# A hybrid decoder layer on one core: a convolution head as a pair in seven products, attention's second halves inside the next pairs, later transposes in block 1

## The chip, the core and the metric

The kernel runs on one core of a Trainium2 chip. The metric is the device time of one execution in microseconds (us). Before the change it is 1216.02 us, the median of three runs (1215.99 to 1218.19).

## The reference

One layer for 512 tokens of 1024 features, all in float32: a feed-forward block, a mixer of two branches (dilated attention and a gated linear recurrence), and a second feed-forward block. Cut to the parts that matter here:

```python
h = h + 0.5 * rms_norm(swiglu(rms_norm(h, g1), w_gate, w_up, w_down), g2)     # first feed-forward block
u = rms_norm(h, mix_norm_pre)
q, k, v, xr, yr, gl = split(u @ w_in)          # 3 x 1536, 1024, 1024, 2048 columns
# attention: 3 groups (dilation 1, 4, 16) of 4 heads of 128; the groups are merged by their log-sum-exp
alpha = softmax(stack(lses), axis=0)
attn_d = einsum('gbsh,gbshe->bshe', alpha, stack(outs)) @ w_attn_branch
# recurrence: causal convolution of width 4 per channel, two gates per head of 256 channels, linear scan
rec_d = (rg_lru_branch(xr, conv_w, conv_b, ...) * gelu(yr)) @ w_rec_branch
gates = sigmoid(gl)
h = h + rms_norm((gates[0] * attn_d + gates[1] * rec_d) @ w_out, mix_norm_post)
h = h + 0.5 * rms_norm(swiglu(rms_norm(h, g3), ...), g4)                      # second feed-forward block
```

## The kernel before

**Precision.** Every large product is made of three matmuls. A weight arrives by DMA in a `raw` buffer, and `split` makes a high half of it on ScalarE (ACT, `L294`) and the remainder, the low half, on VectorE (DVE, `L295`). The activations are split in the same way. High times high, high times low and low times high are added up in PSUM (`L307` to `L309`, or `L677` to `L679` in a pair).

**Pairs in seven products.** Two column blocks of 128 outputs with the same input can be computed as a 2 x 2 block product with seven products in place of eight. Each of the seven has 256 columns, four steps over the features and three matmuls a step: 84 matmuls of 128x256, where the two blocks by themselves take 48 of 128x512. `w_forms` makes the sums of weights that this needs, `seventh` issues one product, `seven` and `seven_on` issue all seven with the evictions that combine them. In `seven` the sums are built outside PSUM, in the order p1, p2, p6, p5, p7, p4, p3; in `seven_on`, in the order p1, p5, p6, p2, p7, p3, p4, several products are built on a copy of an earlier one in PSUM (`copy`, `L691`), so a product can wait for an eviction.

**Stages.** The layer runs through: first feed-forward block; `block1`, which finishes it for one block of 128 tokens at a time (residual, norm statistics, the row `u`, and with `bd1.turn(b)` eight transposes into `um`); the values of attention (`values_first` for group 0, `values_two` for groups 1 and 2 in seven products, whose weight sums are made by `add` at `L1134`); then for each head the three pairs of queries and keys (`qk`, groups 0 to 2) and `attend`; four pairs of output gates; the attention's output product; the recurrence's stage in the order of `LRU_ORDER` (branch 0, branch 1, conv 0, branch 2, gates 0, conv 1, branch 3, ...); the output products; and the second feed-forward block.

**`attend`.** Its first half makes scores, their maxima and exponentials for three groups, and one `exchange` (a masked product, a small matmul with the constant `same` at `L1296`, a masked sum) of group 0's maxima and sums. A row of small VectorE operations makes the weight of each group (`L1304` to `L1315`). The second half begins with a second `exchange` of group 0's weight, scales the exponentials, transposes them (`L1322`) and multiplies them with the values (`om`).

**Conv.** A head has two blocks of 128 channels. Today each is a `gemm` of its own, copied into the padded row `xr` and convolved with four taps (one on ACT, three on DVE).

**Order.** A scheduler puts the instructions of each engine in order by the priority that they had when they were traced; `tc.high_priority(offset)` moves a piece ahead by a number of steps (`AHEAD` 100 for weight loads and splits, `EVAC` 200 for evictions). Each engine then runs its own list in order and waits on semaphores. Weight buffers: `raw` has 2, `w8` (128x1024, both halves) 4, `w4` (128x512) 2. PSUM has 5 tiles `acc` and 3 tiles `aux`. Weights come in the order of `stream_plan`, two 1 MB loads ahead.

Of the kernel before, what the change touches and what calls it, by code (L numbers as in the profile page):

```python
# [10 lines left out]
F32 = mybir.dt.float32  # L11
# [23 lines left out]
EVAC = 200  # L35
NFIRST = 5
# [13 lines left out]
PAIRED = tuple(("branch", h) for h in range(4))  # L50
# [130 lines left out]
def hybrid_layer(ctx: ExitStack, tc: tile.TileContext, xT: bass.AP, xN: bass.AP, wst: bass.AP,  # L181
# [489 lines left out]
    def seventh(t, w, p, ps, start):  # L671
        if len(t[p][0].shape) == 4:
            ps = ps.rearrange("q (b t) -> q b t", b=2)
        for k in range(4):
            ks = slice(k * P, (k + 1) * P)
            wh, wl, xh, xl = w[p][:, 0, ks], w[p][:, 1, ks], t[p][0][:, k], t[p][1][:, k]
            PE.matmul(ps, wh, xh, start=start and k == 0, stop=False, skip_group_check=True)  # L677
            PE.matmul(ps, wh, xl, start=False, stop=False, skip_group_check=True)  # L678
            PE.matmul(ps, wl, xh, start=False, stop=k == 3, skip_group_check=True)  # L679
# [30 lines left out]
    def seven(t, w, z, g, u, seen=lambda ap: ap):  # L710


        b, y = acc_ps()[:, :HB], acc_ps()[:, :HB]

        def product(p, ps, start):
            seventh(t, w, p, ps, start)

        def copy(ps):
            c = tpool.tile([P, HB], F32, name="c", tag="c", bufs=CB)
            with tc.high_priority(offset=EVAC):  # L720
                ACT.activation(c, ps, AF.Copy)  # L721
            return c

        def sum_of(dst, ps, c):
            with tc.high_priority(offset=EVAC):
                DVE.tensor_add(dst, seen(ps), seen(c))
# [339 lines left out]
    def block1(b, sums):  # L1066
        bd1.block(b, sums)
        if b >= 2:
            bd1.turn(b - 2)
# [12 lines left out]
    with ExitStack() as mx:  # L1082
# [16 lines left out]
        def values_first():  # L1099
# [4 lines left out]
            for b in range(4):  # L1104
                bl = slice(b * P, (b + 1) * P)
                for k in range(KC):
                    wh, wl = (w.rearrange("p (k c) -> p k c", k=2)[:, k % 2, :] for w in ws[k // 2])
                    PE.matmul(pss[b], um.hi[k][:, bl], wh, start=k == 0, stop=False)
# [110 lines left out]
        def qk(hd):  # L1219

            q, k = [], []
            for g in range(NG):
                w = pair_of(("pair",) + pairs[hd][g])
                tq, tk = (apool.tile([P, T], F32, name="qk", tag="qk", bufs=QKB) for _ in range(2))
                if g == 0:
                    seven(t, w, acc_ps()[:, :HB], *([nat(x)[:, 2 * i:2 * i + 2] for i in range(2)] for x in (tq, tk)),
                          seen=lambda ap: ap.rearrange("q (p b r) -> q p b r", p=2, b=4))
                else:
                    seven(t, w, acc_ps()[:, :HB], *([x[:, h] for h in HALVES] for x in (tq, tk)))
# [10 lines left out]
        def attend(hd, heads):  # L1240
# [49 lines left out]
            def exchange(dst, src, n):  # L1290
# [5 lines left out]
                PE.matmul(ps, same, x, start=True, stop=True)  # L1296
# [19 lines left out]
            w0 = apool.tile([P, 4, 1], F32, name="w0", tag="w0", bufs=2)  # L1316
            exchange(w0, e[:, 0:1, :], 1)

            def transposed(i, blocks):
                ps, o = aux_ps(), 0  # L1320
                for b in blocks:
                    PE.transpose(ps[:, o:o + P], b, ident)  # L1322
                    o += P
                t = facc[:, i, :]
                ACT.activation(t[:, :o], ps[:, :o], AF.Copy)
                return t

            pts = []
            for g in (1, 2):
                pv = pg[g - 1]  # L1330
                DVE.tensor_mul(pv, pv, e[:, g, :, None].to_broadcast([P, 4, P]))
                pts.append(transposed(3 + g, [pv[:, b, :] for b in range(4)]))
            for b in range(4):
                DVE.tensor_scalar(win[b], win[b], w0[:, b, :], None, op0=ALU.mult)
            ta = transposed(6, [p0[0][:, i * P:(i + 1) * P] for i in range(3)])
            tb = transposed(7, [p0[1][:, i * P:(i + 1) * P] for i in range(4)])
            om = aux_ps()
            for g in (1, 2):
                for b in range(4):
                    PE.matmul(om[:, b * P:(b + 1) * P], vt[g][:, b, :], pts[g - 1][:, b * P:(b + 1) * P],  # L1340
                              start=g == 1 and b == 0, stop=False, skip_group_check=True)
            on = pbr(om)
            for i, (b, j) in enumerate(((0, 0), (1, 0), (1, 1), (2, 1), (2, 2), (3, 2), (3, 3))):
                t = (ta if i < 3 else tb)[:, (i % 3 if i < 3 else i - 3) * P:][:, :P]
                PE.matmul(on[:, :, b, :], vt[0][:, j, :], t.rearrange("q (p r) -> q p r", p=4),
                          start=False, stop=i == 6, skip_group_check=True)
            ACT.activation(attn.hi[hd], om, AF.Copy)
            DVE.tensor_sub(attn.lo[hd], om, attn.hi[hd].bitcast(F32))
# [21 lines left out]
    with ExitStack() as mx:  # L1370
# [48 lines left out]
        def two_tiles(w, g, u):  # L1419

            lo, hi = HALVES

            def up(dst, ps, sign):
                with tc.high_priority(offset=EVAC):
                    ACT.activation(dst[:, lo], ps, AF.Copy, scale=sign)

            def g1(ps, c):
                with tc.high_priority(offset=EVAC):
                    DVE.tensor_add(g[:, hi], ps, c)

            def u1(ps, c):
                with tc.high_priority(offset=EVAC):
                    DVE.scalar_tensor_tensor(u[:, hi], ps, -1.0, c, op0=ALU.mult, op1=ALU.subtract)

            seven_on(t, w, lambda y: up(g, y, 1.0), g1, lambda v: up(u, v, -1.0), u1)

        def conv(hd, then):

            for c in (2 * hd, 2 * hd + 1):
                ps, w = acc_ps(), fetch(("in", 36 + c))  # L1440
                if c % 2:
                    then()
                gemm(ps, w, um)
                xr = lpool.tile([P, 3 + T], F32, name="xr", tag="xr", bufs=2)
                DVE.memset(xr[:, 0:3], 0.0)
                xc = sig[:, c, :]
                with tc.high_priority(offset=EVAC):
                    DVE.tensor_copy(ip(xr[:, 3:]), pi(ps))
# [4 lines left out]
                    split(rec.hi[c], rec.lo[c], xc)  # L1453

        gels, late = {}, []

        def branch(hd):

            gels[hd] = []
            if ("branch", hd) in PAIRED:  # L1460
                w = paired.pop(("branch", hd))
                gels[hd] = [lpool.tile([P, T], F32, name="ge", tag="ge", bufs=8) for _ in range(2)]
                two_tiles(w, *gels[hd])
# [75 lines left out]
        for i, (what, hd) in enumerate(LRU_ORDER):  # L1539
            if i and LRU_ORDER[i - 1] == PAIRED[-1]:  # L1540
# [197 lines left out]
```

## Time and profile before

| | before |
|---|---|
| median of 3 runs | 1216.02 us |
| the profiled execution | 1215.6 us |
| its span, first to last instruction | 1213.8 us |
| granted TensorE clock, mean | 0.998 |
| busy: PE, PEld, DVE, ACT, POOL | 1203.8, 1103.0, 1012.5, 802.5, 26.1 us |
| pair matmuls of 128x256 (`L677` to `L679`) | 3 x 1288 |
| convolution, branch and gate matmuls of 128x512 (`L307` to `L309`) | 3 x 128 |

PE is TensorE's matmul, PEld its weight load, which overlaps it; DVE is VectorE, ACT ScalarE, POOL GpSimd, and SPq the queue of SyncE, which issues most loads. Matmuls are pipelined: a row's duration covers more than the distance to the next row's start, and the distance is what a matmul costs. In a row of the profile "idle before" names the wait that ended last. An `x2` or `x4` behind a row stands for as many instructions of the same kind in succession.

### The profile page before, as it was taken

To read this page: it belongs to the slowest core of one execution; us is meant where nothing else is said; L and a number is where in the kernel's file an instruction comes from. 1 tells how busy PE (TensorE), PEld (TensorE's weight loads), DVE (VectorE), ACT (ScalarE), POOL (GpSimd) and SP (SyncE) were. 2 spreads that over 40 slices of the span, in tenths; PEclk is the share of its full clock that TensorE was granted. 3 is DMA by queue.
4 is the path that set the end of the run, shared out by engine and by line. 5 is a ranking of instruction groups with operands and counts; after the bars stand their busy time and mean duration, and the time that the engine had idled before them with its cause. 6 is when DMAs were issued, how large, how long until landed. Compare 5 with 4: busy or idle time off the path is not lost.

```text
span 1213.8 us, 19596 instructions
## 1 busy us (share of the span) xinstructions
PE 1203.8 (99%) x7838; PEld 1103.0 (91%) x7838; DVE 1012.5 (83%) x1547; ACT 802.5 (66%) x1377; POOL 26.1 (2%) x51
## 2 busy tenths in 40 slices
PE   9999999999999999999999999999999999999997
PEld 8899999999888999999989888888899999999996
DVE  7988888899689888888766899875798888889975
ACT  7556778776566565666735888834566677878752
POOL 0000000000011000000000000000100000000000
PEclk9999999999999999999999999999999999999999
DMA  6223333334635222222222441325443333333341
GB/s 248 102 73 122 122 122 122 122 122 146 242 119 162 70 96 88 79 99 85 100 75 87 144 169 70 105 104 180 149 140 122 122 122 122 122 122 122 139 174 70
DMA packets 29835, 148.75 MB, mean 123 GB/s; under 512 B 3376, under 2 KB 6832, under 8 KB 15792
## 3 DMA queue, kind: packets, MB, share of 16 engines
q1 hardware_dynamic: 22176, 130.04, 30.2%
q0 software_dynamic: 7280, 17.30, 4.3%
q8 instruction: 61, 1.00, 0.3%
q14 instruction: 30, 0.25, 0.1%
q10 hardware_dynamic: 288, 0.17, 0.0%
HBM read 137.01 MB, written 6.29 MB: 118 GB/s over the span
## 4 chain that ended last, share of the span: by engine, by line
PE 92%; DVE 4%; ACT 2%; DMA 1%; issue 1%; DVEq 0%; ACTq 0%
PE acc L677 15%; PE acc L678 15%; PE acc L679 15%; PE acc L308 6%; PE acc L307 6%; PE acc L309 6%; PE aux L946 3%; PE aux L947 3%; PE aux L948 3%; PE acc L423 3%; PE acc L422 3%; PE acc L421 3%; DVE w L295 1%; DMA raw<-in_w 1%; ACT w L294 1%
## 5 line engine op out<-in xcount | busy, mean ns | idle before, releaser
L677 PE MATMUL acc<-big,w 128*128 128x256 f32 x1288 | 365.4, 284 | 0.3 <-ACT c L691 0.3
L678 PE MATMUL acc<-big,w 128*128 128x256 f32 x1288 | 365.4, 284 | 0.0
L679 PE MATMUL acc<-big,w 128*128 128x256 f32 x1288 | 365.0, 283 | 0.0
L295 DVE TENSOR_TENSOR w<-raw,w 128x1024 fp32r<-128x1024 f32 (+1 forms) x274 | 298.9, 1095 | 60.7 <-ACT w L294 55.2
L294 ACT ACTIVATE w<-raw 128x1024 fp32r<-128x1024 f32 (+1 forms) x274 | 260.5, 955 | 98.1 <-PE acc L309 37.8
L677 PEld LDWEIGHTS acc<-big,w 128*128 128x128 f32 x1288 | 246.9, 192 | 2.5 <-ACT c L691 0.9
L678 PEld LDWEIGHTS acc<-big,w 128*128 128x128 f32 x1288 | 246.9, 192 | 1.6
L679 PEld LDWEIGHTS acc<-big,w 128*128 128x128 f32 x1288 | 246.9, 192 | 0.0
L946 PE MATMUL aux<-w,xf 128*128 128x512 f32 x196 | 76.3, 393 | 0.8 <-ACT w L294 0.8
L947 PE MATMUL aux<-w,xf 128*128 128x512 f32 x196 | 76.6, 391 | 0.0
L948 PE MATMUL aux<-w,xf 128*128 128x512 f32 x196 | 76.3, 389 | 0.0
L294 ACT ACTIVATE w<-s 128x1024 fp32r<-128x1024 f32 x53 | 56.1, 1058 | 19.6 <-PE acc L679 15.6
L295 DVE TENSOR_TENSOR w<-s,w 128x1024 fp32r<-128x1024 f32 x53 | 64.6, 1219 | 3.0 <-ACT w L294 2.9
L640 DVE TENSOR_TENSOR s<-raw 128x512 f32<-128x512 f32 x53 | 36.4, 687 | 32.8 <-DMA raw<-in_w 32.8
L691 ACT ACTIVATE c<-acc 128x256 f32<-128x256 f32 x78 | 29.6, 381 | 39.0 <-PE acc L679 38.6
L307 PE MATMUL acc<-big,w 128*128 128x512 f32 x128 | 49.8, 389 | 0.0
L308 PE MATMUL acc<-big,w 128*128 128x512 f32 x128 | 49.8, 389 | 0.0
L309 PE MATMUL acc<-big,w 128*128 128x512 f32 x128 | 49.8, 389 | 0.0
L854 ACT ACTIVATE g<-g 128x256 f32<-128x256 f32 x35 | 14.6, 416 | 50.1 <-DVE g L853 50.1
L721 ACT ACTIVATE c<-acc 128x256 f32<-128x256 f32 x72 | 27.2, 379 | 29.3 <-PE acc L679 27.9
L307 PE MATMUL acc<-xf,w 128*128 128x512 f32 (+1 forms) x136 | 46.3, 343 | 0.0
L309 PE MATMUL acc<-xf,w 128*128 128x512 f32 (+1 forms) x136 | 46.2, 340 | 0.0
(428 smaller groups left out, 2804.3 us busy)
## 6 DMA issues: line engine op xcount, KB each, us to landing
raw<-in_w SPq DMA_DIRECT2D x107, 1024.0 KB, 4.8
raw<-in_w SPq DMA_DIRECT2D x16, 512.0 KB, 3.5
big<-xf POOLq DMA_DIRECT2D x6, 512.0 KB, 3.3
gains<-in_rows POOLq DMA_DIRECT2D x5, 512.0 KB, 5.2
h<-in_x SPq DMA_DIRECT2D x8, 256.0 KB, 4.9
h<-in_xn POOLq DMA_DIRECT2D x4, 512.0 KB, 5.4
kept_m<-h POOLq DMA_DIRECT2D x4, 512.0 KB, 2.9
vals<-in_w SPq DMA_DIRECT2D x2, 1024.0 KB, 7.1
```

The costliest lines, as they stand in the source:

```text
L294: ACT.activation(dh, src, AF.Copy)
L295: DVE.tensor_sub(dl, src, dh.bitcast(F32))
L307: PE.matmul(ps, wh, xh, start=first, stop=False)
L308: PE.matmul(ps, wh, xl, start=False, stop=False)
L309: PE.matmul(ps, wl, xh, start=False, stop=last)
L421: PE.matmul(ps, x.hi[k][:, bl], wh, start=k == 0, stop=False)
L677: PE.matmul(ps, wh, xh, start=start and k == 0, stop=False, skip_group_check=True)
L678: PE.matmul(ps, wh, xl, start=False, stop=False, skip_group_check=True)
L679: PE.matmul(ps, wl, xh, start=False, stop=k == 3, skip_group_check=True)
L946: PE.matmul(ps, xh, wh, start=first and j == 0, stop=False, skip_group_check=True)
L947: PE.matmul(ps, xh, wl, start=False, stop=False, skip_group_check=True)
L948: PE.matmul(ps, xl, wh, start=False, stop=j == 1, skip_group_check=True)
```

## The change

Three edits go together.

1. `PAIRED` gets `("conv", 0)`: both blocks of the convolution's head 0 come from one `seven_on` pair, whose parts are written straight into the two padded rows `xr`; both blocks' taps follow the pair. Conv 1 to 3 stay as they were. The condition on `LRU_ORDER[i - 1]` names `("branch", 3)` outright, so it selects the same place.
2. `attend` returns its second half as the function `rest`, and `seven` calls it in the middle of a later pair by its new argument `then`: head 0's after p1 of group 1 of head 1's pairs, head 1's and 2's after p4 of group 0 of the next head's, head 3's after p4 of the first pair of output gates. The first half is traced at priority offset `FRONT` (60), the second at `BACK` (150), and the second exchange's matmul is issued behind the last product matmul traced so far (`state["last"]`).
3. `block1` calls `bd1.turn(0)` only at block 2, and no longer `turn(1)` at block 3; `values_first` calls `turn(1)`, `turn(2)`, `turn(3)` after the second of eight steps of its blocks 0, 1, 2 (before: `turn(2)` and `turn(3)` in blocks 1 and 2).

```diff
+BACK = 150
+FRONT = 60
...
-PAIRED = tuple(("branch", h) for h in range(4))
+PAIRED = tuple(("branch", h) for h in range(4)) + (("conv", 0),)
...
-            PE.matmul(ps, wl, xh, start=False, stop=k == 3, skip_group_check=True)
+            state["last"] = PE.matmul(ps, wl, xh, start=False, stop=k == 3, skip_group_check=True).ins
...
-    def seven(t, w, z, g, u, seen=lambda ap: ap):
+    def seven(t, w, z, g, u, seen=lambda ap: ap, then={}):
...
             seventh(t, w, p, ps, start)
+            if p in then:
+                then[p]()
...
-        if b >= 2:
-            bd1.turn(b - 2)
+        if b == 2:
+            bd1.turn(0)
...
-                    if k == 1 and 0 < b < 3:
+                    if k == 1 and b < 3:
                         bd1.turn(b + 1)
...
-                PE.matmul(ps, same, x, start=True, stop=True)
+                with tc.issue_after(behind) if behind else nullcontext():
+                    PE.matmul(ps, same, x, start=True, stop=True)
...
-            exchange(w0, e[:, 0:1, :], 1)
+            def rest():
+                with tc.high_priority(offset=BACK):
+                    weighted()
+            def weighted():
+                w0 = apool.tile([P, 4, 1], F32, name="w0", tag="w0", bufs=2)
+                exchange(w0, e[:, 0:1, :], 1, state["last"])
...
         for hd in range(NH):
-            attend(hd, qkvs.pop(hd))
+            with tc.high_priority(offset=FRONT):
+                rest = attend(hd, qkvs.pop(hd))
             if hd + 1 < NH:
-                qkvs[hd + 1] = qk(hd + 1)
+                qkvs[hd + 1] = qk(hd + 1, {0: {"p4": rest}} if hd else {1: {"p1": rest}})
...
             seven(t, pair_of(("pair", 52 + c, 53 + c)), acc_ps()[:, :HB], [g[:, h] for h in HALVES],
-                  [u[:, h] for h in HALVES])
+                  [u[:, h] for h in HALVES], then={} if c else {"p4": rest})
...
+            if ("conv", hd) in PAIRED:
+                then()
+                xrs = [padded() for _ in cs]
+                two_tiles(paired.pop(("conv", hd)), *([ip(xr[:, 3:])[:, 2 * h:2 * h + 2, :] for h in range(2)]
+                                                      for xr in xrs),
+                          seen=lambda ap: ap.rearrange("q (p i) -> q p i", p=2))
+                for c, xr in zip(cs, xrs):
+                    convolved(c, xr)
+                return
```

The order of the instructions moves with it at three places of which the prediction speaks. Line numbers of the changed kernel are 4 to 34 higher (the split is `L298` and `L299`, an eviction in a pair `L695`, the value sums `L1140`, a combination in `seven` `L732`).

VectorE at the beginning of the second values; `w8_3974` is the first weight's low half, `vals` the weight sums, `big_4029` and `rb_4025` forms of the activations. Before:

```order
L617 SCALAR_TENSOR_TENSOR ts_3987<-facc_79,ts_3986 128x1024
L618 TENSOR_TENSOR facc_79<-facc_79 128x2x512
L295 TENSOR_TENSOR big_4029<-ts_3986,big_4029 128x1024
L295 TENSOR_TENSOR rb_4025<-ts_3987,rb_4025 128x1024
L295 TENSOR_TENSOR w8_3974<-raw_3960,w8_3974 128x1024
L1134 TENSOR_TENSOR vals_3790<-vals_3964,vals_3966 128x1024
L295 TENSOR_TENSOR w8_3980<-raw_3962,w8_3980 128x1024
```

Now:

```order
L621 SCALAR_TENSOR_TENSOR ts_3987<-facc_79,ts_3986 128x1024
L622 TENSOR_TENSOR facc_79<-facc_79 128x2x512
L299 TENSOR_TENSOR big_4029<-ts_3986,big_4029 128x1024
L1140 TENSOR_TENSOR vals_3774<-vals_3964,vals_3966 128x1024 x2
L299 TENSOR_TENSOR w8_3974<-raw_3960,w8_3974 128x1024
L299 TENSOR_TENSOR w8_3980<-raw_3962,w8_3980 128x1024
```

Both sums of the value weights now stand ahead of the first low half, and the split of `rb_4025` has moved behind it.

VectorE at the second exchange of head 1; `e`, `d` and `tot` are the small operations on the groups' weights, `xch` is the exchange's operand, `qk` a combination of the pair that runs at the time, `facc` the scaled exponentials. Before:

```order
L726 TENSOR_TENSOR qk_5222<-acc_5224,c_5266 128x2x4x32
L1307 TENSOR_TENSOR e_5138<-nm_5135,st_5088 128x12
L645 TENSOR_TENSOR raw_5323<-s12_5325,raw_5323 128x512
L1310 TENSOR_TENSOR d_5141<-e_5138,st_5088 128x12
L1312 TENSOR_TENSOR tot_5143<-d_5141 128x4
L1313 TENSOR_TENSOR tot_5143<-tot_5143,d_5141 128x4
L1314 RECIPROCAL tot_5143<-tot_5143 128x4
L1315 TENSOR_TENSOR e_5138<-e_5138,tot_5143 128x12
L295 TENSOR_TENSOR w4_5332<-raw_5323,w4_5332 128x512
L726 TENSOR_TENSOR qk_5342<-acc_5346,c_5359 128x256
L1293 TENSOR_TENSOR xch_5149<-e_5138,cst_76 128x4x4
L1331 TENSOR_TENSOR facc_79<-facc_79,e_5138 128x512
```

Now:

```order
L299 TENSOR_TENSOR w8_5156<-raw_5148,w8_5156 128x1024
L732 TENSOR_TENSOR qk_5168<-c_5239,c_5225 128x2x4x32
L1318 TENSOR_TENSOR d_5141<-e_5138,st_5088 128x12
L732 TENSOR_TENSOR qk_5168<-acc_5171,c_5239 128x2x4x32
L1320 TENSOR_TENSOR tot_5143<-d_5141 128x4
L1321 TENSOR_TENSOR tot_5143<-tot_5143,d_5141 128x4
L1322 RECIPROCAL tot_5143<-tot_5143 128x4
L1323 TENSOR_TENSOR e_5138<-e_5138,tot_5143 128x12
L299 TENSOR_TENSOR w8_5329<-raw_5323,w8_5329 128x1024
L732 TENSOR_TENSOR qk_5167<-acc_5169,c_5211 128x2x4x32
L1300 TENSOR_TENSOR xch_5255<-e_5138,cst_76 128x4x4
L1344 TENSOR_TENSOR facc_79<-facc_79,e_5138 128x512
```

Two low halves of 128x1024 now stand around the small operations, where one of 128x512 stood behind them, and one more combination stands among them.

ScalarE at the beginning of branch 1; `ge_6836` and `ge_6837` are branch 0's rows, `acc_6940` or `acc_6958` is the copy on which branch 1's third product builds, and the weights named `raw_7041` before and `raw_6936` now are those of the next step in `LRU_ORDER`. Before:

```order
L294 ACTIVATE w8_7043<-raw_7041 128x1024
L1425 ACTIVATE ge_6837<-acc_6841 128x256
L1476 ACT_TABLE_LOAD
L1476 ACTIVATE ge_6836<-ge_6836 128x512
L691 ACTIVATE acc_6940<-acc_6938 128x256
```

Now:

```order
L298 ACTIVATE w8_6939<-raw_6936 128x1024
L1441 ACTIVATE ge_6837<-acc_6841 128x256
L298 ACTIVATE w4_6938<-raw_6936 128x512
L1510 ACT_TABLE_LOAD
L1510 ACTIVATE ge_6836<-ge_6836 128x512
L695 ACTIVATE acc_6958<-acc_6956 128x256
```

One split of 128x512 has moved ahead of the load of the Gelu's table. The orders of POOL and SyncE are as before.

More of the change, by code (lines that the diff above doesn't have):

```diff
@@ L1217, in pair_of, with qk @@
             return forms.pop(key)
-        def qk(hd):
+        def qk(hd, then={}):
             q, k = [], []
@@ L1226, in qk @@
                     seven(t, w, acc_ps()[:, :HB], *([nat(x)[:, 2 * i:2 * i + 2] for i in range(2)] for x in (tq, tk)),
-                          seen=lambda ap: ap.rearrange("q (p b r) -> q p b r", p=2, b=4))
+                          seen=lambda ap: ap.rearrange("q (p b r) -> q p b r", p=2, b=4), then=then.get(g, {}))
                 else:
-                    seven(t, w, acc_ps()[:, :HB], *([x[:, h] for h in HALVES] for x in (tq, tk)))
+                    seven(t, w, acc_ps()[:, :HB], *([x[:, h] for h in HALVES] for x in (tq, tk)),
+                          then=then.get(g, {}))
                 q.append(tq)
@@ L1287, in attend, with exchange @@
                 pg.append(pv)
-            def exchange(dst, src, n):
+            def exchange(dst, src, n, behind=None):
                 x = apool.tile([P, 4, 2, 4], F32, name="xch", tag="xch", bufs=2)[:, :, :n, :]
@@ L1328, in attend @@
[L1328 to L1336, printed above, removed]
@@ L1337, in attend @@
-            om = aux_ps()
-            for g in (1, 2):
-                for b in range(4):
[L1340 to L1346, printed above, removed]
@@ L1453, in conv @@
                     split(rec.hi[c], rec.lo[c], xc)
+            cs = (2 * hd, 2 * hd + 1)
+            if ("conv", hd) in PAIRED:
[7 more added lines that the diff above has]
+                return
+            for c in cs:
+                ps, w = acc_ps(), fetch(("in", 36 + c))
+                if c % 2:
+                    then()
+                gemm(ps, w, um)
+                xr = padded()
+                with tc.high_priority(offset=EVAC):
+                    DVE.tensor_copy(ip(xr[:, 3:]), pi(ps))
+                convolved(c, xr)
         gels, late = {}, []
@@ L1539, in hybrid_layer @@
         for i, (what, hd) in enumerate(LRU_ORDER):
-            if i and LRU_ORDER[i - 1] == PAIRED[-1]:
+            if i and LRU_ORDER[i - 1] == ("branch", 3):
                 rec_t = rec_half()
```

62 lines of the change are left out of this document (38 added, 24 removed).

## The prediction

> **What bounds the kernel.** I read the page first, then the timeline of each engine around the three places that the change touches. In the page the first row gives each engine's busy time, the second the share of the span in the chain of work that ended last.
>
> ```profile
> PE 1203.8 (99%) x7838; PEld 1103.0 (91%) x7838; DVE 1012.5 (83%) x1547; ACT 802.5 (66%) x1377; POOL 26.1 (2%) x51
> PE 92%; DVE 4%; ACT 2%; DMA 1%; issue 1%; DVEq 0%; ACTq 0%
> ```
>
> TensorE is the bound nearly everywhere. So there are two ways to change the time: fewer or shorter matmuls, or a change in the few tenths for which TensorE waits. I price both from the start-to-start distances of matmuls, since the durations in the rows overlap. First the cost of a product, from PE's timeline around head 3's second exchange (the matmul of L1296); start, duration, engine, line:
>
> ```profile
> 567.80 0.28 PE L679 MATMUL acc<-big,w 128*128 128x256 f32 x1
> ...
> 575.72 0.28 PE L679 MATMUL acc<-rb,w 128*128 128x256 f32 x1
> 576.08 0.37 PE L1296 MATMUL aux<-xch,cst 128*128 128x16 f32 x2
> 576.29 0.37 PE L677 MATMUL acc<-rb,w 128*128 128x256 f32 x1
> 576.50 0.28 PE L678 MATMUL acc<-rb,w 128*128 128x256 f32 x1
> ```
>
> From 567.80 to 575.72 there are 66 gaps of 256-column products: 0.12 us each. The exchange should have started at 575.84 and started at 576.08, so it waits 0.24 us; I take the same for the other three heads. Around block 1 and the values PE shows two more waits:
>
> ```profile
> 346.19 0.39 PE L1108 MATMUL acc<-w,big 128*128 128x512 f32 x1
> 346.81 0.66 PE L511 MATMUL aux<-cst,u 128*128 128x128 f32 x4 [0.23 <-DVE u L503]
> ...
> 348.26 0.40 PE L1108 MATMUL acc<-w,big 128*128 128x512 f32 x1
> ```
>
> ```profile
> 371.50 0.39 PE L1149 MATMUL aux<-w,big 128*128 128x512 f32 x1
> ...
> 374.64 0.50 PE L1149 MATMUL aux<-w,big 128*128 128x512 f32 x1 [0.26 <-DVE w L295]
> ```
>
> Three 512-column matmuls and eight transposes lie between 346.19 and 348.26; at 0.227 (next fence) and about 0.11 each they need 1.57 us, so 0.5 us is waiting. Between 371.50 and 374.64 lie 12 matmuls, 2.72 us, and 0.42 us of waiting.
>
> **The convolution of head 0.** PE's timeline at its first matmul and at the first of branch 2:
>
> ```profile
> 649.71 0.40 PE L307 MATMUL acc<-big,w 128*128 128x512 f32 x1
> ...
> 660.62 0.28 PE L677 MATMUL acc<-big,w 128*128 128x256 f32 x1
> ```
>
> Its 48 matmuls take 10.91 us (0.227 each). The pair has seven products of 12 matmuls: 84 x 0.12 = 10.08. That is **-0.83 us** on the path, if TensorE does not wait. [...]
>
> What the pair adds on DVE is four adds and one more split of 512 columns, and its taps all come after the pair. DVE is 83% busy, and I find no product that waits for these. But ACT's order changes at the start of branch 1. ACT's rows there, and PE's first matmul of branch 1's third product:
>
> ```profile
> 640.16 1.28 ACT L1476 ACT_TABLE_LOAD   x1
> 641.46 0.63 ACT L1476 ACTIVATE ge<-ge 128x512 f32<-128x512 f32 x1
> 641.99 0.37 ACT L691 ACTIVATE acc<-acc 128x256 f32<-128x256 f32 x1
> ...
> 644.29 0.63 ACT L294 ACTIVATE w<-raw 128x512 fp32r<-128x512 f32 x1 [1.12 <-DMA raw<-in_w]
> ```
>
> ```profile
> 642.41 0.39 PE L677 MATMUL acc<-rb,w 128*128 128x256 f32 x1
> ```
>
> The eviction at 641.99 ends at 642.36 and lets TensorE begin branch 1's third product at 642.41, so it has no slack today. In the changed order the conv pair's 512-column split stands ahead of the table load (its weights come in the same load as the split before it, so it need not wait as at 644.29). It takes 0.63, about 0.54 from start to start (641.46 to 641.99 for an operation of that size): everything behind it, the eviction too, comes 0.54 later. **+0.54 us** (0 if the split were hidden, 0.7 if its full length counts).
>
> In branch 2 the first taps and copies into `xr` stand in ACT's order ahead of the eviction that its third product needs. Evictions, two 0.81 us scalings and half copies add up to an end 0.15 us before it is wanted if a strided half copy costs as much as a plain one (0.38), and 0.25 us after if it costs 0.2 more. With a second such place at the seventh product, which waits behind a 1.06 us split: 0 to 0.6, I take **+0.3**.
>
> **Block 1 and the values.** Transposes that today follow the first matmul of the values now follow the sixth: 5 x 0.227 = 1.1 us later, which covers the 0.5 wait. The later two pairs of transposes stay covered, since DVE's two rows of `h` now go ahead of two splits of 0.6 and all statistics come 0.5 to 0.9 earlier. But DVE's order behind them puts both sums of the value weights (L1134) ahead of the first weight split. These sums read two loads that are issued when the last `u` is done. DVE's last `u`; SP's issue; the loads' shortest, median and longest time to landing (two of them); and DVE's order today:
>
> ```profile
> 359.66 1.41 DVE L503 SCALAR_TENSOR_TENSOR u<-h,stat,gains 128x512 f32<-128x512 f32 x2
> 361.15 0.80 SPq L239 DMA_DIRECT2D vals<-in_w  x2
> DMA to landing us min/median/max: 5.2/7.1/8.9
> 369.96 1.21 DVE L295 TENSOR_TENSOR w<-raw,w 128x1024 fp32r<-128x1024 f32 x1
> 371.10 1.21 DVE L1134 TENSOR_TENSOR vals<-vals 128x1024 f32<-128x1024 f32 x1
> ```
>
> Today the second load, issued about 361.5, lands near 361.5 + 8.9 = 370.4, just ahead of its first reader at 371.10. In the changed kernel the last `u` ends about 0.8 earlier, so the load lands near 369.6, while DVE is at the sum by 368.0 (369.96, less one split of 1.14 that moves behind, less 0.8). It waits. Then come two sums at 1.14 and the split itself, 1.21 with 0.1 to PE: TensorE's first low matmul starts at 369.6 + 3.6 = 373.2. It would be due at 371.50 - 0.5 = 371.0, and ran at 371.50. So +1.7 there, of which the 0.42 at 374.64 comes back, since the later split then is in time: **+1.3 us**. Bounds: if the loads land by 368.0, the split is in time within 0.6 and the part wins 0.35; if the second takes 0.7 longer to land, +2.0.
>
> **Attention.** The second exchange moves behind the first product of the next pair but one (head 0) or the next pair. What sets it is a chain on DVE and ACT that starts when the fourth product of the pair before ends. ACT's eviction and split, and DVE's small steps up to the exchange's operand, from today's rows:
>
> ```profile
> 567.88 0.36 ACT L721 ACTIVATE c<-acc 128x256 f32<-128x256 f32 x1
> 568.15 1.05 ACT L294 ACTIVATE w<-raw 128x1024 fp32r<-128x1024 f32 x1
> ...
> 576.94 0.38 ACT L721 ACTIVATE c<-acc 128x256 f32<-128x256 f32 x1 [0.86 <-PE acc L679]
> ```
>
> ```profile
> 573.94 0.16 DVE L1310 TENSOR_TENSOR d<-e,st 128x12 f32<-128x12 f32 x1
> ...
> 575.43 0.42 DVE L726 TENSOR_TENSOR g<-acc,c 128x256 f32<-128x256 f32 x1
> 575.77 0.16 DVE L1293 TENSOR_TENSOR xch<-e,cst 128x16 f32<-128x16 f32 x1
> ```
>
> Step by step: eviction 0.20 after its product's end (576.94, where 576.50 plus two gaps is 576.74), 0.27 to the split, 1.08 for it, 1.14 for DVE's low half, 0.33 for a combination, then the small steps: 573.94 to 575.43 is 1.49, less the 0.60 of a split between, and with one more combination in place of a gap, 1.12. Then a second low half, 1.14, a combination, 0.34, and 0.31 from the exchange's operand to PE (575.77 to 576.08): 5.93 us. TensorE needs 48 x 0.12 = 5.76 for the four products in between. So the exchange still waits 0.17 instead of 0.24: 4 x 0.07, **-0.3 us**. Bounds: -1.0 if the whole wait goes; +0.5 if each step of the chain slips by a few hundredths. Transposes behind it keep 0.1 to 0.3 of slack by the same count, and the scores, now between products of the third pair, about as much.
>
> **The sum**: -0.83 + 0.54 + 0.3 + 1.3 - 0.3 = +1.0 us. The profiled execution took 1215.6 (span 1213.8 and 1.8 around it), 0.4 below the median of 1216.02. With the median as the base: **1217.0 us**, +0.08%. A measurement of this kernel can tell about 0.2%, 2.4 us, from no change, so I forecast no change: between 1213.6 and 1218.4.
>
> **Rivals.**
> *The loads land in time* (by 368.0). Then the values win 0.35 instead of losing 1.3: 1215.4. For it: one load took 5.2. Against it: the second took 8.9, and both move 2 MB at once.
> *All waits go.* With the loads in time and the exchange ready (another -0.7) it is 1214.65; with branch 1's split hidden (-0.54) 1214.1, with branch 2 free too (-0.3) 1213.8, with the conv pair at its lower bound (0.119 a matmul, -0.1) 1213.7, and if one late wait of the LRU as long as block 1's goes too (-0.5) 1213.2. For it: each wait is a few tenths long. Against it: all must go at once.
> *Slower: TensorE pays for each change between score matmuls and products.* Scores and exchange stand in three groups per head today and in about ten in the new order, 28 more changes in all. After the exchange's group, the next gap is 0.21 (576.29 to 576.50 in the rows above) and not 0.12. If these 0.09 come with every change, it is 28 x 0.09 = 2.5: 1219.5. It decides from 0.05 a change on. Against it stands a lone transpose:
>
> ```profile
> 578.93 0.27 PE L1322 MATMUL aux<-cst,facc 128*128 128x128 f32 x1
> 578.95 0.37 PE L679 MATMUL acc<-big,w 128*128 128x256 f32 x1
> 579.15 0.60 PE L1322 MATMUL aux<-cst,facc 128*128 128x128 f32 x4
> ```
>
> Transpose and product take 0.22 together, 0.12 and 0.10: no more than a transpose in a group. A score matmul has two passes, and none stands alone today.
> *Slower: the value loads land 1.5 us later still*, 1218.5.
> *Slower: short matmuls are dearer in the convolution.* At 0.15 each instead of 0.12, the 84 cost 2.5 more: 1219.5. Against it stand the 66 gaps of 0.12 above. [...]
>
> **Chances.** Forecast as worked out 0.54, loads in time 0.18, all waits gone 0.14, changes on TensorE 0.10, late loads 0.03, dearer short matmuls 0.01. All waits gone lies below 1213.6 in 0.10 of its 0.14; with 0.02 for the lower ends of the other cases: faster 0.12. Slower: 0.10, 0.02 of the late loads, 0.01, and 0.07 for the upper ends of my bounds together: 0.20. Same: 0.68. The range from 1213.4 to 1219.6 takes in both rivals and leaves out their far ends.
>
> **What would show it.** Right: in the changed profile the first low matmul of the second values waits for DVE about 2 us; DVE idles 1 to 2 us on the value loads; the four exchanges still show a gap of some 0.3 before them; branch 1's third product starts 0.5 late behind an eviction; conv 0 takes 10.1 us. Wrong: if PE runs through 368 to 376 without a gap, the values term fails and the time falls by 1.7; if 256-column products next to lone scores stand 0.2 apart with no wait, the rival of the changes holds. A kernel faster than 1213.6 would mean that the chain of 5.93 us and the loads are both mispriced.

## The result, and the profile after

The changed kernel takes 1219.32 us, the median of 20 runs (1217.61 to 1221.42); the kernel before, run beside it, takes 1217.16 us (20 runs, 1215.48 to 1218.42). The ratio is 1.002, with a 95% interval of 1.0013 to 1.0026: slower by 2.4 us (1.6 to 3.2) as a ratio, by 2.2 between the medians. As a ratio that is at the upper edge of what the prediction calls no change; the time itself is 0.3 us below the upper end of its range.

The profiled execution took 1221.42 us, the longest of the 20, so its 5.8 us over the profile of before (1215.6) are not the price of the change. The page's rows of busy time and of the chain that ended last:

```profile
PE 1206.1 (99%) x7874; PEld 1106.4 (91%) x7874; DVE 1016.0 (83%) x1553; ACT 804.1 (66%) x1384; POOL 26.0 (2%) x51
PE 87%; DVE 6%; ACT 4%; DMA 2%; issue 1%; DVEq 0%; SPq 0%; ACTq 0%
```

TensorE is still the bound, but 5 points of the chain have gone to VectorE, ScalarE and the DMA: waits. To place them I took the start of each stage's first matmul from PE's timeline of both kernels and subtracted. The last column is a second profile of the same changed kernel, 1217.80 us, one of the runs below.

| stage, us | before | after | after, second profile |
|---|---|---|---|
| up to the first values (same work but for block 1) | 346.19 | 347.64 | 346.46 |
| first values, with block 1's transposes | 25.08 | 24.44 | 24.44 |
| second values | 38.63 | 42.26 | 40.20 |
| pairs, attention, output gates | 197.74 | 198.16 | 197.31 |
| attention's output product | 21.78 | 21.79 | 21.79 |
| branch 0, branch 1, conv 0, branch 2, gates 0 | 46.73 | 46.80 | 46.80 |
| conv 1, branch 3, gates 1 | 26.94 | 27.68 | 27.67 |

**The second values.** PE's timeline and then VectorE's, with the time from issue to landing of the two value loads (shortest, median, longest):

```profile
372.08 0.39 PE L1154 MATMUL aux<-w,big 128*128 128x512 f32 x1
374.75 0.50 PE L1155 MATMUL aux<-w,big 128*128 128x512 f32 x1 [2.28 <-DVE w L299]
375.08 0.54 PE L1156 MATMUL aux<-w,big 128*128 128x512 f32 x1
375.42 0.63 PE L1154 MATMUL aux<-w,big 128*128 128x512 f32 x1
375.85 0.63 PE L1155 MATMUL aux<-w,big 128*128 128x512 f32 x1
376.28 0.63 PE L1156 MATMUL aux<-w,big 128*128 128x512 f32 x1
```

```profile
368.12 1.22 DVE L299 TENSOR_TENSOR big<-ts,big 128x1024 fp32r<-128x1024 f32 x1
371.20 2.36 DVE L1140 TENSOR_TENSOR vals<-vals 128x1024 f32<-128x1024 f32 x2 [1.87 <-DMA vals<-in_w]
373.48 4.62 DVE L299 TENSOR_TENSOR w<-raw,w 128x1024 fp32r<-128x1024 f32 x4
DMA to landing us min/median/max: 5.0/7.1/9.2
```

VectorE reaches the two sums and waits 1.87 us for the second load, then makes both sums, and only then the first low half. TensorE starts its first low matmul 2.67 us after the high one; 0.23 is usual. What follows was not forecast: from 375.42 on, matmuls of 128x512 start 0.43 apart in place of 0.227. The windows of that stretch give the granted clock (the column behind POOL):

```profile
374.80:375.20 0.40, 0.40 (x2) 0.36 (x3) 0.40 (x1) 0.00 (x0) 0.40 (x2) 0.97 0.00 0
375.20:378.40 3.20, 3.20 (x9) 2.45 (x8) 3.20 (x4) 0.00 (x0) 0.93 (x2) 0.50 0.35 82
378.40:378.80 0.40, 0.40 (x3) 0.35 (x2) 0.40 (x1) 0.00 (x0) 0.00 (x0) 0.76 0.00 0
```

The clock is 0.50 for 3.4 us. The second profile has a pause of 2.17 and no halved clock; the two differ by 2.06 us in this stage, 0.50 for the shorter pause and some 1.55 for the clock.

**Branch 1, and an exchange.** PE's timeline at branch 1's third product, ScalarE's there, and PE's at head 3's second exchange:

```profile
647.12 0.28 PE L683 MATMUL acc<-big,w 128*128 128x256 f32 x1
647.79 0.39 PE L681 MATMUL acc<-rb,w 128*128 128x256 f32 x1 [0.39 <-ACT acc L695]
```

```profile
644.90 0.62 ACT L298 ACTIVATE w<-raw 128x512 fp32r<-128x512 f32 x1
645.54 1.28 ACT L1510 ACT_TABLE_LOAD   x1
646.84 0.63 ACT L1510 ACTIVATE ge<-ge 128x512 f32<-128x512 f32 x1
647.37 0.36 ACT L695 ACTIVATE acc<-acc 128x256 f32<-128x256 f32 x1
```

```profile
578.13 0.28 PE L683 MATMUL acc<-big,w 128*128 128x256 f32 x1
578.40 0.40 PE L1304 MATMUL aux<-xch,cst 128*128 128x16 f32 x2
```

The split of 128x512 stands ahead of the table load, and TensorE waits 0.55 (647.79 less 647.24). The exchange comes 0.15 late, where it was 0.24. The convolution's pair begins with the first of these rows, and branch 2 with the second:

```profile
655.08 0.28 PE L681 MATMUL acc<-big,w 128*128 128x256 f32 x1
...
665.16 0.28 PE L681 MATMUL acc<-big,w 128*128 128x256 f32 x1
```

**Branch 3.** ScalarE's timeline of before, then of after, and the wait on PE in after:

```profile
689.50 0.37 ACT L691 ACTIVATE acc<-acc 128x256 f32<-128x256 f32 x1
689.89 1.28 ACT L1529 ACT_TABLE_LOAD   x1
...
692.74 0.38 ACT L691 ACTIVATE c<-acc 128x256 f32<-128x256 f32 x1
694.22 0.63 ACT L294 ACTIVATE rec<-sig 128x512 fp32r<-128x512 f32 x1 [1.10 <-DVE sig L1451]
```

```profile
696.39 0.38 ACT L695 ACTIVATE c<-acc 128x256 f32<-128x256 f32 x1 [1.04 <-PE acc L683]
696.79 1.28 ACT L1563 ACT_TABLE_LOAD   x1
...
699.10 0.63 ACT L298 ACTIVATE rec<-sig 128x512 fp32r<-128x512 f32 x1 [0.38 <-DVE sig L1465]
699.63 0.37 ACT L695 ACTIVATE c<-acc 128x256 f32<-128x256 f32 x1
```

```profile
699.43 0.28 PE L681 MATMUL acc<-big,w 128*128 128x256 f32 x1
700.05 0.39 PE L681 MATMUL acc<-big,w 128*128 128x256 f32 x1 [0.34 <-ACT c L695]
```

Before, a table load went into the gap behind branch 3's first copy, and the third copy went ahead of a split that waits for the convolution's taps. Now ScalarE first waits for the second copy, loads the table after it, and makes the third copy behind that split. A wait of 0.50 on TensorE is new, and the wait for the first gate's input grows from 0.40 to 0.55. No step of the prediction looked here.

### The profile page after: what moved, and what is told of

Read it like the earlier page. It is cut to its first block, busy times and chain, and to the rows that moved or that the text cites. A ratio compares the mean times of both kernels' runs of the same rounds, so it can differ in the third digit from the quotient of the medians.

```text
span 1219.6 us, 19688 instructions
## 1 busy us (share of the span) xinstructions
PE 1206.1 (99%) x7874; PEld 1106.4 (91%) x7874; DVE 1016.0 (83%) x1553; ACT 804.1 (66%) x1384; POOL 26.0 (2%) x51
## 4 chain that ended last, share of the span: by engine, by line
PE 87%; DVE 6%; ACT 4%; DMA 2%; issue 1%; DVEq 0%; SPq 0%; ACTq 0%
PE acc L681 14%; PE acc L682 14%; PE acc L683 14%; PE acc L311 6%; PE acc L312 6%; PE acc L313 5%; PE aux L952 4%; PE aux L953 3%; PE aux L954 3%; PE acc L426 2%; PE acc L425 2%; PE acc L427 2%; DVE w L299 1%; ACT w L298 1%; DMA raw<-in_w 1%
## 5 line engine op out<-in xcount | busy, mean ns | idle before, releaser
L681 PE MATMUL acc<-big,w 128*128 128x256 f32 x1308 | 371.5, 284 | 0.7 <-ACT c L695 0.7
L682 PE MATMUL acc<-big,w 128*128 128x256 f32 x1308 | 371.5, 284 | 0.0
L683 PE MATMUL acc<-big,w 128*128 128x256 f32 x1308 | 370.8, 283 | 0.0
L299 DVE TENSOR_TENSOR w<-raw,w 128x1024 fp32r<-128x1024 f32 (+1 forms) x276 | 300.1, 1093 | 66.7 <-ACT w L298 53.7
L298 ACT ACTIVATE w<-raw 128x1024 fp32r<-128x1024 f32 (+1 forms) x276 | 261.9, 954 | 86.3 <-PE acc L313 36.3
L681 PEld LDWEIGHTS acc<-big,w 128*128 128x128 f32 x1308 | 250.7, 192 | 3.1 <-ACT c L695 1.5
L682 PEld LDWEIGHTS acc<-big,w 128*128 128x128 f32 x1308 | 250.7, 192 | 1.5
L683 PEld LDWEIGHTS acc<-big,w 128*128 128x128 f32 x1308 | 250.8, 192 | 0.0
L298 ACT ACTIVATE w<-s 128x1024 fp32r<-128x1024 f32 x53 | 56.1, 1058 | 21.7 <-PE acc L683 17.6
L299 DVE TENSOR_TENSOR w<-s,w 128x1024 fp32r<-128x1024 f32 x53 | 64.6, 1219 | 3.8 <-ACT w L298 3.5
L695 ACT ACTIVATE c<-acc 128x256 f32<-128x256 f32 x80 | 30.6, 382 | 42.0 <-PE acc L683 41.5
L681 PE MATMUL acc<-rb,w 128*128 128x256 f32 x168 | 48.9, 291 | 0.4 <-ACT acc L695 0.4
L682 PE MATMUL acc<-rb,w 128*128 128x256 f32 x168 | 48.6, 289 | 0.0
L683 PE MATMUL acc<-rb,w 128*128 128x256 f32 x168 | 48.2, 287 | 0.0
```

The lines of the kernel that those rows point to most:

```text
L298: ACT.activation(dh, src, AF.Copy)
L299: DVE.tensor_sub(dl, src, dh.bitcast(F32))
L683: state["last"] = PE.matmul(ps, wl, xh, start=False, stop=k == 3, skip_group_check=True).ins
```

## The experiments

**The three edits apart.** Each of the next three kernels is the kernel before with one edit; beside them runs the changed kernel with VectorE's order at the second values turned.

*The third edit alone* (`turns_only`):

```diff
-        if b >= 2:
-            bd1.turn(b - 2)
+        if b == 2:
+            bd1.turn(0)
...
-                    if k == 1 and 0 < b < 3:
+                    if k == 1 and b < 3:
```

> The kernel before with the third edit alone (block 1's transposes later). Theory A (the loss is made at the second values: VectorE waits 1.9 us for the value loads, TensorE pauses for about 2.7 us, and its clock then halves for some 3.4 us): values_first 0.6 shorter, the second values 3.6 longer, about +3.0 us, ratio near 1.0025; the profile shows the pause and a granted clock near 0.5 for 3 us behind it. Rival B (the halved clock belongs to that one execution): the pause is there, the clock stays at 1.0, about +1.3 us, ratio near 1.001. Rival C (the loss is in attention or the recurrence): ratio at or below 1.000.

Measured: 1219.18 us against 1217.36, ratio 1.0018 (1.0009 to 1.0027). First values 24.44, second values 40.33. The pause in PE's timeline and the windows around it:

```profile
371.87 0.39 PE L1148 MATMUL aux<-w,big 128*128 128x512 f32 x1
374.22 0.50 PE L1149 MATMUL aux<-w,big 128*128 128x512 f32 x1 [1.96 <-DVE w L295]
```

```profile
372.00:374.00 2.00, 0.26 (x2) 0.00 (x0) 2.00 (x2) 1.67 (x3) 0.04 (x1) 1.00 0.33 70
374.00:376.00 2.00, 1.78 (x8) 1.49 (x9) 2.00 (x3) 0.00 (x0) 1.94 (x4) 1.00 0.29 66
```

This edit makes the pause by itself, and it is most of the loss. The pause is 2.35 and the clock stays at 1.00: in this execution theory A's second half did not happen. The ratio lies between A's 1.0025 and B's 1.001; how often the clock falls is taken up below. Rival C falls.

*The second edit alone* (`attn_only`): the changed kernel with the `turns_only` diff reversed and

```diff
-PAIRED = tuple(("branch", h) for h in range(4)) + (("conv", 0),)
+PAIRED = tuple(("branch", h) for h in range(4))
```

> The kernel before with the second edit alone (attention's second halves in the next pairs). Theory A: within 0.5 us of before, ratio 0.9997 to 1.0004; the four second exchanges wait 0.15 to 0.2 each, as before, and one score matmul of the last head waits about 0.6. Rival C (TensorE pays for each change between scores and products): +2 us or more, ratio 1.0016 or higher.

Measured: 1217.81 against 1217.36, ratio 1.0001 (0.9993 to 1.001). Pairs, attention and gates take 197.35 in place of 197.74, 0.4 less; no score matmul waits, nor does one in the three further profiles of the changed kernel below, so the 0.60 for which TensorE sat idle before one of them in the first profile was an accident of that execution. A price of 2 us for the changes between scores and products is excluded.

*The first edit alone* (`conv_only`): the changed kernel with the `turns_only` diff reversed and attention as before:

```diff
-            with tc.high_priority(offset=FRONT):
-                rest = attend(hd, qkvs.pop(hd))
+            attend(hd, qkvs.pop(hd))()
...
-                qkvs[hd + 1] = qk(hd + 1, {0: {"p4": rest}} if hd else {1: {"p1": rest}})
+                qkvs[hd + 1] = qk(hd + 1)
...
-                with tc.high_priority(offset=BACK):
-                    weighted()
+                weighted()
...
-                exchange(w0, e[:, 0:1, :], 1, state["last"])
+                exchange(w0, e[:, 0:1, :], 1)
...
-                  [u[:, h] for h in HALVES], then={} if c else {"p4": rest})
+                  [u[:, h] for h in HALVES], then={})
```

> The kernel before with the first edit alone (head 0's convolution as a pair). Theory A: the pair takes 10.1 us in place of 10.9, branch 1's third product waits 0.5 for its eviction, and branch 3 waits about 0.5 for another eviction and 0.15 more for its first gate: together 0.8 us slower, ratio near 1.0007. Rival (the prediction's sum for this edit, without branch 3): 0.0 us, ratio 1.0000, and no wait in branch 3.

Measured: 1217.90 against 1217.36, ratio 1.0007 (0.9998 to 1.0016). Branch 0 to gates 0 take 46.80 (+0.07), conv 1 to gates 1 28.24 (+1.30): branch 3 waits 0.50 for its third copy, and the first gate waits 1.12 for a split of `rec`, where it waited 0.40 (0.15 more was expected). The rival's sum without branch 3 is too low. The interval still touches 1.000; the placed waits carry the verdict.

*VectorE's order turned* (`sums_behind`), the changed kernel with the sums behind the four low halves of the first two weights (`low` is a low half's instruction) and two splits of the activations' forms behind the second of them, not behind all four as the expectation says:

```diff
+                        state.setdefault("lows", []).append(low)
...
+            with tc.issue_after(state["lows"][1]) if name in ('p6', 'p7') else nullcontext():
+                split(v[:, 0], v[:, 1], src)
...
             steps[0]()
-            add(sd, u0, u1)
+            with tc.issue_after(state["lows"][3]):
+                add(sd, u0, u1)
```

> The changed kernel with VectorE's order at the second values turned: both sums of the value weights, and two splits of the activations' forms, follow all four low halves of the first two weights. Theory A: no pause, clock at 1.0, the second values 3.6 us shorter than in the changed kernel's profile; against before about +0.2 to +0.6 us, ratio near 1.0003. Rival B: the same place, but a gain of 1.9 us only, and the change would still be 0.0005 or more above before. Rival C: no gain, ratio 1.002.

Measured: 1217.65 against 1217.36, ratio 1.0001 (0.9992 to 1.0009). PE's timeline at the place of the pause:

```profile
372.50 0.39 PE L1157 MATMUL aux<-w,big 128*128 128x512 f32 x1
372.73 0.39 PE L1158 MATMUL aux<-w,big 128*128 128x512 f32 x1
```

No pause: the second values take 38.64, as before the change, and the first keep their gain of 0.64. Against the changed kernel's 1.002 the ratio falls by 0.002, some 2.3 us, and the change's loss is gone. The mechanism, sums that wait for loads ahead of the first low half, is shown by making it (`turns_only`) and by taking it away.

**The clock.** *The pause filled with work* (`fill10`):

```diff
+                        if idle is not None and j == 0 and k == 0:
+                            for _ in range(10):
+                                PE.matmul(idle, xh, wh, start=True, stop=True, skip_group_check=True)
...
-            prod("p1", w1, b, True)
+            prod("p1", w1, b, True, y[0])
```

> The changed kernel with ten more matmuls of 128x512 behind the first matmul of the second values, into a PSUM tile that is free then: TensorE works through its pause, and VectorE's wait for the value loads stays. Theory A (the pause lets the clock fall, in this run or that): the first low matmul comes at the same distance as in the changed kernel, 2.4 to 2.7 us behind the first, the clock stays at 1.0 after it; time below the changed kernel's by the share of executions with a halved clock, 0 to 1.9 us: ratio to before 1.0005 to 1.0018. Rival (the clock falls for another reason, such as the loads): halved for 3 us although TensorE was busy, ratio 1.002.

Measured: 1221.72 against 1216.92, ratio 1.0042 (1.0028 to 1.0055), above both expectations. The mean granted clock of the profiled execution is 0.999, and the first low matmul comes 2.52 us behind the high one. But this kernel isn't a clean trial. PE's rows, at the second values and in the second feed-forward block:

```profile
376.32 0.50 PE L1158 MATMUL aux<-w,big 128*128 128x512 f32 x1 [0.61 <-DVE w L299]
...
1063.91 0.39 PE L681 MATMUL acc<-big,w 128*128 128x256 f32 x1 [1.53 <-ACT acc L695]
```

The first is a wait for the second low half, 0.77, that the changed kernel's order of matmuls covers. The second follows a weight load that landed late, in this execution: ScalarE's split of it waited 2.82 us, to 1062.26. With the first the stage is 41.41; about 2 us of the median stay unexplained. On the clock a single profile decides little, since it doesn't always fall with the pause either, as the next profiles show. But none of this kernel's five runs shows a mean clock below 0.998, where nine of the changed kernel's 20 do; so nothing here speaks for the rival.

*A longer pause* (`sums_twice`), both sums made twice and ahead of the first low half:

```diff
-            w1, w2 = form(g0), form(g1)
             steps[0]()
-            add(sd, u0, u1)
+            for _ in range(2):
+                add(sd, u0, u1)
+            with tc.issue_after(state["sum"]):
+                w1, w2 = form(g0), form(g1)
```

> The changed kernel with both sums of the value weights made twice ahead of the first low half: TensorE's pause grows by 2.3 to about 4.9 us. If a longer pause always halves the clock: granted clock near 0.5 for about 3.4 us behind it, and 2.3 + 1.0 to 1.9 us more than the changed kernel, ratio to before 1.0045 to 1.0055. If the halved clock was an accident of one execution: clock 1.0, ratio near 1.0037.

Measured: 1222.67 against 1216.92, ratio 1.0049 (1.0036 to 1.0061). The windows:

```profile
372.80:373.20 0.40, 0.00 (x0) 0.00 (x0) 0.40 (x2) 0.00 (x0) 0.40 (x2) 0.79 0.00 0
373.20:379.60 6.40, 4.27 (x10) 3.40 (x11) 6.40 (x6) 0.00 (x0) 1.23 (x3) 0.50 0.17 41
379.60:380.00 0.40, 0.40 (x2) 0.30 (x2) 0.21 (x1) 0.00 (x0) 0.00 (x0) 0.68 0.00 0
```

With a pause of 4.71 the granted clock is 0.50 for 6.8 us, twice as long as in the first profile and twice what was expected. The stage takes 44.88: of the 4.68 over the second profile of the changed kernel, 2.54 are the longer pause, and the other 2.1 fit the slower matmuls behind it. The mean clocks of its five runs are 0.996 (three), 0.997 and 0.998.

*The changed kernel once more*, three times without an edit:

> The changed kernel as it is, one more profile: whether the clock halves behind the pause in every execution (Theory A: pause of 2.4 to 2.7 us and clock near 0.5 for 3 us) or only in some (clock 1.0 behind the same pause). The wait of one score transpose of the last head (0.76 in the first profile) should be gone if it was an accident.

> The changed kernel as it is, a third profile. If the time that the loads take decides: a pause of under 2.5 us goes with a clock of 1.0, one of over 2.6 with a clock of 0.5 for 3.4 us. [...]

> The changed kernel as it is, a fourth profile, for the same question as the third: how long the pause is, and whether the clock halves for 3.4 us behind it.

Measured: 1217.80, 1221.63 and 1218.48 us, with pauses of 2.17, 2.18 and 2.85 us, and a second values' stage of 40.20, 40.23 and 40.90. The clock is 1.00 in all three. The last has a longer pause than the first profile's 2.67, and its clock did not fall:

```profile
371.29 0.39 PE L1154 MATMUL aux<-w,big 128*128 128x512 f32 x1
374.14 0.50 PE L1155 MATMUL aux<-w,big 128*128 128x512 f32 x1 [2.46 <-DVE w L299]
```

```profile
371.20:374.20 3.00, 0.54 (x4) 0.11 (x2) 3.00 (x4) 1.87 (x3) 1.66 (x4) 1.00 0.35 81
374.20:376.00 1.80, 1.80 (x8) 1.49 (x9) 1.80 (x2) 0.00 (x0) 1.14 (x3) 1.00 0.56 128
376.00:378.00 2.00, 2.00 (x11) 1.58 (x10) 2.00 (x3) 0.07 (x1) 0.00 (x0) 1.00 0.06 16
```

So the length of the pause alone does not decide between 2.2 and 2.9 us; what else does was not shown. The pause is in every profile of this kernel, the halved clock in one of four. Its share over all executions can be estimated from the mean clock that is on record for each run. In the profiled execution of the kernel before and in ten of the changed kernel and its variants (all but the first profile, 0.997, and `sums_twice`, 0.996) this mean is 0.998 or 0.999, and 3.41 us at half clock take off 0.0014. Of the changed kernel's 20 runs nine have 0.997 (median 1219.78 us, the other eleven 1218.65), and so have five of the eleven of `turns_only`, the five longest. None of the 63 runs of the kernel before that stood beside the experiments has less than 0.998, and none of the 55 runs without the pause (`attn_only`, `conv_only`, `sums_behind`, and `evict_first` and `evict_again` below). By this estimate the clock falls behind this pause in about half of the executions; a mean that is listed as 0.998 can hide a halved stretch, so nine of 20 may be too few.

**Three orders turned** (`evict_first`, and once more as `evict_again`): the turned order of the sums, and on ScalarE

```diff
-            with tc.high_priority(offset=EVAC):
-                ACT.activation(dst, ps, AF.Copy)
+            with tc.high_priority(offset=300):
+                state["copied"] = ACT.activation(dst, ps, AF.Copy).ins
...
         copy(b, y)
+        state["first copy"] = state["copied"]
...
-                    ACT.activation(ge, ge, AF.Gelu_apprx_tanh)
+                    with tc.issue_after(state["first copy"]) if hd < 2 else nullcontext():
+                        ACT.activation(ge, ge, AF.Gelu_apprx_tanh)
```

> The kernel of the turned VectorE order (sums behind the low halves) with two more orders on ScalarE: branch 0's Gelu table load follows the eviction for branch 1's third product, and a pair's copies get priority 300 in place of 200, so that branch 3's third copy stands ahead of a split. Theory A: branch 1's wait of 0.5 and branch 3's of 0.5 go, 1.1 to 1.2 us below the kernel of the turned order alone, ratio to before 0.9990 to 0.9995. Rival (the evictions would be late anyway, behind other work of ScalarE): ratio 1.0000, and the waits stand with another operation ahead of the eviction.

> The kernel of the three turned orders (sums behind the low halves, Gelu behind the eviction, copies at priority 300) once more, for a narrower interval: ratio to before 0.9990 to 0.9995 if the gains of its stages hold (values -0.64, attention -0.4, branches and convolution -0.6, conv 1 to branch 3 +0.3); 1.0000 if the first comparison was luck.

Measured: 1215.94 against 1216.92, ratio 0.9991 (0.9982 to 1.0000), and 1215.69 against 1216.60, ratio 0.9990 (0.9981 to 0.9999). ScalarE's timeline at branch 1 and PE's in branch 3, in the second of them:

```profile
641.82 0.37 ACT L696 ACTIVATE acc<-acc 128x256 f32<-128x256 f32 x1 [0.48 <-PE acc L684]
642.20 1.28 ACT L1516 ACT_TABLE_LOAD   x1
```

```profile
696.48 0.39 PE L682 MATMUL acc<-rb,w 128*128 128x256 f32 x1 [0.55 <-ACT acc L696]
```

At branch 1 the copy is ahead of the table load, and branch 0 to gates 0 take 46.16, 0.64 less. In branch 3 the wait for the third copy is gone, but a later copy is now waited for with 0.70, so conv 1 to gates 1 take 27.22 and not 26.94: the rival holds for half of that place. By both ratios this version is about 1 us faster than the kernel before, though the intervals end at 1.0000 and 0.9999, and some 3.5 us faster than the changed one.

## Why the prediction held, and where it did not

- **The second values** were named as the place and VectorE's order as the cause, and the first low matmul waits for VectorE as described. The forecast was +1.3 us for block 1 and the values. Without the halved clock the second values take 40.20 to 40.90 (+1.6 to +2.3), the first 0.64 less: +0.9 to +1.6. The loads landed after 8.7 to 9.3 us, as today's 8.9 said. One term was missing: that TensorE can come out of the pause at half its clock (0.50 for 3.41 us in the first profile, none in the other three). In the first profile that adds some 1.55 us, and by the mean clocks it happens in about half of the executions.
- **The convolution**: the pair runs from 655.08 to 665.16, 10.08 us, to the hundredth the 84 x 0.12 of the sum. Branch 1's wait was put at 0.54 and is 0.55; branches 0 and 1 together take 0.50 more. Branch 2 with gates 0 was put at +0.3 and takes 0.40 more (15.93 in place of 15.53). The whole part was put at 0.0 and is +0.07, and here the terms are right, not only their sum.
- **Attention**: the exchange was to wait 0.17 and waits 0.15 to 0.20 (before 0.17 to 0.24); the part was put at -0.3 and is -0.4 in the kernel with this edit alone, -0.3 to -0.4 in the three further profiles. The four waits fall from 0.90 to 0.69 together, so they give 0.2 of it; the rest is not placed.
- **Conv 1 to branch 3** is the step that failed: the sum has no term for it. It costs 0.74 in three of the four profiles of the changed kernel, and 1.3 in the other and in `conv_only`. The prediction followed ScalarE's order to the end of branch 2, and the order that the pair moves goes on into branch 3.
- **The sum**: +1.0 was forecast. Put together anew: +1.2 for the values, about 0.7 for the clock (1.55 us in nine of 20 runs), 0.1, 0.9 and -0.4 make +2.5, where 2.4 was measured (1.6 to 3.2). The two terms that the forecast lacked, the clock and conv 1 to branch 3, make 1.6 us of this. The range held, but in part by luck: its upper end of 1219.6 was set for a rival, TensorE's price for changes, that the runs exclude. The base had also moved: before was 1216.02 in the three runs that stand ahead of the prediction and 1217.16 in the twenty.
- Of the rivals, TensorE's price for changes is excluded by `attn_only`, dearer short matmuls by the pair's 10.08 (no run shows the 0.15 us of that rival; the 84 take 0.12 each), and the loads were never in time.

## What to carry to other kernels

Where a scheduler sets the order, look on each in-order engine for the first instruction that waits for a load, and for what stands behind it that another engine needs next: two sums that only the third product needs, 48 matmuls of 0.227 later, kept TensorE waiting some 2 us because the one urgent split stood behind them. An edit that speeds one stage can move table loads and copies a stage and more downstream (in branch 3 here, for 0.74 us), so the order has to be compared up to where both orders agree again. A single profile can be 2 us off the median in a kernel of 1200; a repeat of the same kernel told which of its waits belonged to the change.

## What the runs showed of the hardware

Behind a pause of 2.67 us TensorE's granted clock was 0.50 in one execution, and behind one of 2.85 us it stayed at 1.00 in another; with a pause of 4.71 us it was 0.50 for longer. The windows give the halved stretch its length: 375.18 to 378.59 from the shares 0.97 and 0.76 of the windows at its ends, 3.41 us, and 373.03 to 379.86 in the kernel with the longer pause, 6.83, twice that. There the clock fell while TensorE still waited: the matmul that ended the pause began at 375.33. In the first profile all 2.28 us of idleness lie in the 3.41 us ahead of the halved stretch:

```profile
371.77:375.18 3.41, 1.13 (x6) 0.63 (x5) 3.41 (x4) 2.09 (x3) 2.16 (x6) 1.00 0.36 88
375.18:378.59 3.41, 3.41 (x10) 2.64 (x9) 3.41 (x4) 0.00 (x0) 0.95 (x2) 0.50 0.33 77
```

The first figure behind the length is TensorE's busy time. In the fourth profile (its windows stand above) TensorE idles for 2.46 us and the clock stays at 1.00, and so it does behind the pauses of the second and third profile (2.17 and 2.18) and of `turns_only` (2.35). Behind the wait of 1.53 us at 1063.91 in `fill10` the next matmul takes the usual 0.28. So more idleness than the first profile's was not always followed by half the clock, and no run here tells what decides.

Executions of one and the same kernel also differ ahead of the changed stages: the first values of the changed kernel began at 346.46, 346.85, 347.64 and 349.64 us in its four profiles, and the work up to there is the same. In the last of these VectorE waited 3.02 us, to 311.33, for ScalarE's half of a split, and TensorE 0.80 us, to 311.63, for a copy; in the first profile VectorE waited 1.45 us for the same split, to 308.82, and ScalarE 0.30 us for its load.
